# Neighbourhood attention in column order: 416 keys for each query tile, values permuted through a DRAM scratch

## The chip, the cores and the metric

The kernel runs on one core of a Trainium2 chip, as one launch. A core has five engines with instruction queues of their own: TensorE (PE; its weight loads are listed apart as PEld), VectorE (DVE), ScalarE (ACT), GpSimd (POOL) and SyncE (SP). Matmuls write PSUM, which the kernel divides into eight banks of 128 x 512 fp32; everything else lies in SBUF or in DRAM. Transfers are issued from SP's queue and, fewer, from ACT's. The metric is the device time of one execution in microseconds, as the median of several runs.

## The reference

A two-layer diffusion backbone on 256 latent tokens and 256 context tokens of width 2048. Layer 0 projects both through one wide matrix and runs 16 heads of two-dimensional neighbourhood attention beside a bidirectional state-space (SSD) mixer of 8 groups; both are gated, concatenated (4096 wide) and projected back. Layer 1 is a gated short convolution. The part that the change touches is the attention:

```python
rows = seq // GRID_W                       # 256 / 64 = 4 rows of 64 columns
kh = min(NA_KH, rows)                      # 4: every row is in the window
col_start = jnp.clip(col - NA_KW // 2, 0, GRID_W - NA_KW)          # NA_KW = 16
in_win = (col[None, :] >= col_start[:, None]) & (col[None, :] < col_start[:, None] + NA_KW)
...
s_lat = jnp.einsum('bqhd,bkhd->bhqk', qr, kb) * scale + bias        # bias from rpb: row and column distance
s_lat = jnp.where(mask, s_lat, -jnp.inf)
s_ctx = jnp.einsum('bqhd,bkhd->bhqk', qr, k_ctx) * scale
pr = jax.nn.softmax(jnp.concatenate([s_lat, s_ctx], axis=-1), axis=-1)
out = pr[..., :latent] @ vb + pr[..., latent:] @ v_ctx
```

A query in column c sees all four rows of 16 columns around c, and all 256 context tokens. Tokens are numbered row by row: token = 64 * row + column.

## The kernel before

**Precision.** Matrix products are made of three passes: each operand is split into a high part, rounded to the format that TensorE reads fast (fp32r), and the remainder, and high x high, high x low and low x high are added in one bank. `mm` (line 195) issues a matmul, `turn` (line 199) a transpose by a matmul against the identity. Weights come from DRAM in pieces of 512 KB into one of five `raw` buffers (lines 381, 383, on SP), ACT rounds a piece to its high part (line 420), DVE subtracts for the low part (line 427) and frees the buffer; three places hold split weights ahead of TensorE.

**The order of the work.** The program is generated by a planner (class `Plan`): every emitted instruction advances a model of each engine's time. The projections are emitted in a fixed order as the main line of TensorE. All else is generators in three lists, `urgent`, `side` and `back`. A generator yields what it needs next (an engine, the data, a number of banks), and `pump` resumes it when the model says that this would be ready; `may` demands for TensorE that the data be due 0.7 us before the model's present (800 ns less 100), so that matmuls of the side work stand in TensorE's queue only where they should not have to wait. Every engine works its queue in the order emitted, so a wrong guess of the model is a real wait. The model books a DMA at 450 ns of the issuing queue; it lands, from SP, after 1000 ns, its bytes at 270 a ns and 1000 ns more, and from ACT after 1000 ns, its bytes and 2500 ns. A task also needs room in a budget of nine 128 x 512 temporaries.

**The attention.** Heads come in four groups `a` of four. Projections of Q, K, gate and V of a group are followed by those of an SSD group pair: for groups 1 and 2 the order is Q, K, gate, V, SSD, and for group 3 it is Q, K, SSD, gate, V, and then the output projection. Group 0's K and V are summed over eight stages at the start, V in place in `Vt` (line 789).

- `kq_gen`: per 128 tokens, norm, transpose into a bank (4 heads x 128 tokens), ACT writes the high part to `KT` or `QT` (lines 994, 998), DVE the low part to `KL` or `QL` (lines 996, 1000). `KT` and `KL` hold, for each head, 256 latent and then 256 context tokens.
- `v_gen`: when the heads of the group before are done, copies V of the 512 tokens from four banks to `Vt` (line 1012).
- `head_gen`, one for each head: loads the head's bias (four DMAs from a DRAM table `rpbs`, which one DMA builds before, line 929), adds the column mask (line 1044), and for each of two query tiles of 128 tokens scores all 512 keys (three matmuls of 512 columns), adds bias and takes the maximum (line 1057), exponentiates with the sum (line 1062), and scales (lines 1066, 1067). Then it transposes the probabilities, splits them into `PH` and `PL` (lines 1099, 1101), waits for V and the gate, splits its 128 columns of V (`VH`, line 1110, `VL`, line 1112), runs 12 matmuls of 256 columns, and multiplies by the gate (line 1122). `PH` and `PL` exist once, so a head transposes only after the value product of the head before.
- `put_mix` keeps the result for the output projection: in a DRAM scratch `mixd`, or, late in the kernel, at once as split tiles (lines 944, 946). `mix_gen` loads from the scratch and splits (lines 1557, 1561, 1562).

The first pass of the output projection reads 16 pairs of such results with two column blocks, 24 matmuls of 512 columns a pair, in the order 0 to 5, 8 to 15, 6, 7: the last SSD group is pair 15 and comes fourteenth, the heads of group 3 are pairs 6 and 7 and come last.

Of the kernel before, what the change touches and what calls it, by code (L numbers as in the profile page):

```python
# [141 lines left out]
def kernel(ctx: ExitStack, tc, x, cx, ada0, w0, adaT, w_in, w_out, sc_in, sc_out, rpb, small, const,  # L142
# [15 lines left out]
    def drt(shape, name):  # L158
        return dr.tile(list(shape), F32, name="dram_" + name)
# [48 lines left out]
    def spawn(q, gen, tmps=0, halves=0):  # L208
        q.append(Task(gen, tmps, halves))
# [142 lines left out]
    ident, strip, mask, mhalf = C_("ident"), C_("strip"), C_("mask"), C_("mhalf")  # L352
# [561 lines left out]
    got.add(("V", 0))  # L914
# [43 lines left out]
    attn = [0]  # L958

    def kq_gen(key, a, ps, nt, stat, dst, low, banked):  # L960
# [23 lines left out]
        for t in range(nt):  # L984
# [7 lines left out]
            if key == "K":  # L992
                give(free_t, kns[t])
                E(S.copy(dst[:, :, o], four(pt)))
                yield W_("DVE", dst[:, :, o])
                E(V.tensor_tensor(out=low[:, :, o], in0=four(pt), in1=dst[:, :, o].bitcast(F32), op=ALU.subtract))
            else:
                E(S.mul(dst[:, :, o], four(pt), gqk))
                yield W_("DVE", dst[:, :, o])
                E(V.scalar_tensor_tensor(out=low[:, :, o], in0=four(pt), scalar=gqk, in1=dst[:, :, o].bitcast(F32),  # L1000
                                         op0=ALU.mult, op1=ALU.subtract))
                give(free_t, kns[t])
# [3 lines left out]
    def v_gen(a, ps):  # L1006
# [7 lines left out]
        got.add(("V", a))  # L1014
# [14 lines left out]
    b0 = rpbs[0, :, :]  # L1029
# [3 lines left out]
    def head_gen(a, h):  # L1033
# [4 lines left out]
        for r in range(4):  # L1038
            E(DMA.dma_start(bt[64 * (r % 2):64 * (r % 2) + 64, r // 2, :].rearrange("p (a b) -> p a b", a=4),
                            bass.AP(tensor=b0.tensor, offset=b0.offset + hd * 64 * 320 + (7 - r) * 31 - 61,  # L1040
                                    ap=[[319, 64], [31, 4], [1, 64]])))
        yield W_("DVE", bt)
        bv = bt[:, 0:2, :].rearrange("p q (r c) -> p (q r) c", c=64)
        E(V.tensor_tensor(out=bv, in0=bv, in1=mask.unsqueeze(1).to_broadcast([128, 8, 64]), op=ALU.add))
        sps = {}

        def score(qt):
            ps = bank()
            o = slice(qt * 128, (qt + 1) * 128)
            mm(ps, QT[:, h, o], KT[:, h, :], True, False)  # L1050
            mm(ps, QT[:, h, o], KL[:, h, :], False, False)
            mm(ps, QL[:, h, o], KT[:, h, :], False, True)
            return ps

        def top(qt, ps):
            sp = sps[qt] = tmp()
            E(V.tensor_tensor_reduce(out=two(sp), in0=two(ps), in1=bt[:, 1:3, :] if qt else bt[:, 0::2, :], scale=1.0,
# [57 lines left out]
        for kt in range(4):  # L1115
            mm(po[:, :256], VH[:, kt], PH[:, kt, :], kt == 0, False)
            mm(po[:, :256], VH[:, kt], PL[:, kt, :], False, False)
            mm(po[:, :256], VL[:, kt], PH[:, kt, :], False, kt == 3)
# [3 lines left out]
        E(V.tensor_tensor(out=o, in0=po[:, :256], in1=gt[:, h, :], op=ALU.mult))  # L1122
# [358 lines left out]
    Btm[0] = st([128, 2, 4, 128], "Btm", name="Btmt")  # L1481
    spawn(urgent, kq_gen("K", 0, parK, 4, statk, KT, KL, False), 4)
# [570 lines left out]
```

## Time and profile before

| | |
|---|---|
| median of 3 runs | 1762.85 us (1761.52 to 1763.02) |
| profiled execution | 1760.31 us, of which the span of instructions is 1758.5 us |
| PE busy | 1736.7 us, 99% |
| PEld busy | 1463.1 us, 83% |
| DVE busy | 1223.6 us, 70% |
| ACT busy | 773.4 us, 44% |
| DMA | 377.66 MB, mean 215 GB/s |
| granted TensorE clock | 0.999 |

In the rows, `L195` is line 195 of the kernel; a group reads line, engine, operation, `out<-in` by the program's names without buffer numbers, shapes, count, then busy us and the mean duration in ns, then the engine's idle time before the group and what ended it. A row of waits gives the total, the number and the longest wait in us. A row of a timeline or of the chain gives the start in us from the span's start, the length in us, and the work. In rows of DMA issues the last number is the median time in us from issue to landing; `SPq` and `ACTq` are the sequencers that issue.

### The profile page before, as it was taken

Reading aid. Unit: us, or ns where it says so; the run is one execution under the profiler, and the core shown is the slowest. Engines: PE = TensorE matmul, PEld = TensorE weight load, DVE = VectorE, ACT = ScalarE, POOL = GpSimd, SP = SyncE. Lnnn points to the kernel's source line nnn. Section 1 sums busy time; section 2 is a strip of 40 time slices with the busy share of each in tenths; the row PEclk is TensorE's granted clock in tenths of the full one; section 3 lists DMA queues with packets and bytes.
Section 4 is the critical chain, followed back from the end, with each engine's and each line's share of the span. In section 5 each row is a group of like instructions: output and inputs, shape, how many; then the busy total and the mean of one; then the engine's idle time right before and its main releaser. Section 6 shows DMA issues by size and latency. Waiting matters only on the chain.

```text
span 1758.5 us, 25025 instructions
## 1 busy us (share of the span) xinstructions
PE 1736.7 (99%) x9451; PEld 1463.1 (83%) x9451; DVE 1223.6 (70%) x1978; ACT 773.4 (44%) x1330; POOL 31.6 (2%) x28
## 2 busy tenths in 40 slices
PE   6999999999999999999999999999999999999998
PEld 4777988889888889888888898888888888888887
DVE  5666887878685878686877787787668555555554
ACT  5333544445242436343435343564446444444442
POOL 0000100001000000000000000000000000000000
PEclk9999999999999999999999999999999999999999
DMA  9987644686756767656776557768767666666563
GB/s 362 342 307 258 209 143 138 183 246 191 234 165 195 219 205 227 210 175 210 220 213 193 166 185 255 246 221 284 274 222 228 195 188 192 192 191 188 190 208 121
DMA packets 202536, 377.66 MB, mean 215 GB/s; under 512 B 32384, under 2 KB 69040, under 8 KB 202416
## 3 DMA queue, kind: packets, MB, share of 16 engines
q1 hardware_dynamic: 195152, 369.49, 65.5%
q10 hardware_dynamic: 7264, 6.58, 1.1%
q8 instruction: 74, 1.21, 0.3%
q14 instruction: 46, 0.38, 0.1%
HBM read 370.62 MB, written 6.71 MB: 215 GB/s over the span
## 4 chain that ended last, share of the span: by engine, by line
PE 94%; DMA 2%; DVE 2%; issue 1%; ACT 0%; POOL 0%; SPq 0%; ACTq 0%; DVEq 0%; POOLq 0%
PE bank L195 91%; PE bank L199 3%; DMA tmp<-dram_csr 1%; DVE w L427 1%; DMA raw<-in_ada 0%; DMA tmp<-dram_exr 0%; DMA raw<-in_adaT 0%; DVE tmp L1235 0%; ACT w L420 0%; POOL statk L572 0%; DVE mix L1562 0%; SPq L583 0%; DVE raw L823 0%; DVE tmp L603 0%; DVE Vt L1012 0%
## 5 line engine op out<-in xcount | busy, mean ns | idle before, releaser
L420 ACT CAST w<-raw 128x1024 fp32r<-128x1024 f32 x343 | 359.5, 1049 | 530.4 <-PE bank L195 447.7
L427 DVE TENSOR_TENSOR w<-raw,w 128x1024 fp32r<-128x1024 f32 x343 | 416.6, 1217 | 231.4 <-ACT w L420 230.1
L195 PE MATMUL bank<-hH,w 128*128 128x256 f32 (+1 forms) x2064 | 488.0, 324 | 1.2 <-DVE w L427 1.1
L195 PE MATMUL bank<-w,hH 128*128 128x512 f32 x1280 | 407.4, 396 | 2.7 <-ACT hH L757 2.5
L195 PEld LDWEIGHTS bank<-hH,w 128*128 128x128 f32 x2064 | 344.7, 188 | 34.2 <-DVE w L427 2.1
L195 PE MATMUL bank<-hL,w 128*128 128x256 f32 (+1 forms) x1040 | 334.3, 321 | 0.0
L195 PEld LDWEIGHTS bank<-w,hH 128*128 128x128 f32 x1280 | 237.7, 189 | 54.4 <-issue 4.0
L195 PE MATMUL bank<-w,hL 128*128 128x512 f32 x640 | 249.9, 391 | 0.1
L195 PEld LDWEIGHTS bank<-hL,w 128*128 128x128 f32 x1040 | 196.3, 189 | 14.9
L195 PE MATMUL bank<-w,h 128*128 128x512 f32 x768 | 179.7, 390 | 0.0
L823 DVE CUSTOM_DVE_ANT_0 raw<-raw,csb 128x1024 f32<-128x1024 f32 x128 | 155.4, 1219 | 26.2 <-DMA raw<-in_adaT 24.0
L195 PEld LDWEIGHTS bank<-w,h 128*128 128x128 f32 x768 | 143.6, 188 | 29.6
L195 PEld LDWEIGHTS bank<-w,hL 128*128 128x128 f32 x640 | 120.5, 188 | 25.4 <-DVE hL L763 0.6
L195 PE MATMUL bank<-w,mix 128*128 128x512 f32 x588 | 138.3, 391 | 0.9 <-DVE w L427 0.9
L195 PEld LDWEIGHTS bank<-w,mix 128*128 128x128 f32 x588 | 109.5, 188 | 24.0 <-DVE w L427 1.3
L1235 DVE SCALAR_TENSOR_TENSOR tmp<-bank,cwh,tmp 128x508 f32<-128x508 f32 (+1 forms) x96 | 71.0, 744 | 1.8
L195 PE MATMUL bank<-KL,h 128*128 128x512 f32 x264 | 63.8, 389 | 0.0
L427 DVE TENSOR_TENSOR KL<-raw,KL 128x1024 fp32r<-128x1024 f32 x32 | 39.1, 1223 | 33.1 <-ACT KL L420 33.1
L427 DVE TENSOR_TENSOR wL<-raw,wH 128x1024 fp32r<-128x1024 f32 x31 | 37.9, 1224 | 33.5 <-ACT wH L420 33.4
L427 DVE TENSOR_TENSOR QL<-raw,QT 128x1024 fp32r<-128x1024 f32 x32 | 39.2, 1224 | 29.8 <-ACT QT L420 29.8
L195 PEld LDWEIGHTS bank<-KL,h 128*128 128x128 f32 x264 | 49.5, 188 | 10.2
L195 PE MATMUL bank<-QT,h 128*128 128x512 f32 x168 | 56.2, 391 | 0.0
(291 smaller groups left out, 1984.7 us busy)
## 6 DMA issues: line engine op xcount, KB each, us to landing
raw<-in_w_in SPq DMA_DIRECT2D x196, 512.0 KB, 3.9
raw<-in_adaT SPq DMA_DIRECT2D x128, 512.0 KB, 4.8
raw<-in_sc_in SPq DMA_DIRECT2D x128, 512.0 KB, 3.8
raw<-in_w_out SPq DMA_DIRECT2D x64, 512.0 KB, 5.0
raw<-in_ada SPq DMA_DIRECT2D x34, 512.0 KB, 6.9
raw<-in_sc_out SPq DMA_DIRECT2D x32, 512.0 KB, 4.1
PT<-in_ada SPq DMA_DIRECT2D x16, 512.0 KB, 6.9
raw<-in_w SPq DMA_DIRECT2D x16, 512.0 KB, 6.1
```

What stands on the lines that cost most here:

```text
L195: E(T.matmul(o, l, r, start=start, stop=stop, skip_group_check=True))
L199: E(T.transpose(o, i, ident if k == 128 else ident[:k, :k]))
L420: E(S.copy(H, v))
L427: E(V.tensor_tensor(out=Lo, in0=v, in1=H.bitcast(F32), op=ALU.subtract))
L823: E(V.tensor_tensor_reduce(out=raw, in0=raw, in1=csb, scale=1.0, scalar=0.0, op0=ALU.mult, op1=ALU.add, accum_out=gp[:, h, m:m + 1]))
L1235: E(V.scalar_tensor_tensor(out=do, in0=di, scalar=cwh[:, 32 * k + ch:32 * k + ch + 1], in1=do, op0=ALU.mult, op1=ALU.add))
```

## The change

Attention sees the tokens column by column: position = 4 * column + row. A tile of 128 queries is then 32 columns of the grid, not two rows. The 32 columns of tile 0 have windows in columns 0 to 39, those of tile 1 in columns 24 to 63. Keys are laid out as 128 positions of columns 0 to 31, 256 context tokens, and 128 positions of columns 32 to 63, so that each tile's keys are one run of 416: positions 0 to 415, or 96 to 511. What is outside gets probability zero by a memset.

- `kq_gen` writes K and Q to their positions: ACT and DVE read a transposed tile and write elements four apart (two pieces for a latent K tile; DVE in two pieces for a Q tile).
- V has tokens on partitions, so its permutation goes through DRAM: `turn_v` writes the two latent tiles to a scratch `vd` with four DMAs on ACT's queue, waits, and reads them back in the new order with one DMA on SP's queue. Only then is V marked as ready.
- The bias comes as a ready table of 128 x 672 a head from the host (an input with the same numbers in another order), with one DMA a head in place of four; the DRAM table `rpbs`, its DMA and two memsets go. The mask is added in three places where columns can be outside the window.
- The value product multiplies the same four key blocks in another order; the gate product reads its result with a stride of four, which puts tokens back in row order.

```diff
@@ constants @@
-for _name, _w in (("ident", 128), ("sel", 2), ("mhalf", 32), ("strip", 384), ("mask", 64)):
+for _name, _w in (("ident", 128), ("sel", 2), ("mhalf", 16), ("mid", 16), ("strip", 384), ("mask", 64)):
@@ after the first stage, group 0 @@
-    got.add(("V", 0))
...
-    rpbs = drt([16, 64, 320], "rpbs")
-    E(DMA.dma_start(rpbs, bass.AP(tensor=rpb.tensor, offset=76, ap=[[465, 16], [0, 64], [1, 320]])))
+    vd = drt([256, 512], "vd")
     dcol = P_("dcol")
-    for b_ in bias:
-        E(G.memset(b_[:, 2, :], 0.0))
...
+    def columns(ap, t):
+        return ap.rearrange("p h (c r) -> p h r c", r=4)[:, :, 2 * t:2 * t + 2, :]
+
+    def turn_v(a):
+        for t in range(2):
+            for r in range(2):
+                yield W_("AQ", Vt[:, t, :])
+                E(DMA2.dma_start(vd.rearrange("(c r) n -> c r n", r=4)[:, 2 * t + r, :], Vt[64 * r:64 * r + 64, t, :]))
+        yield W_("SP", vd)
+        E(DMA.dma_start(Vt[:, 0:2, :], vd.rearrange("(t p) n -> p t n", p=128)))
+        got.add(("V", a))
@@ kq_gen @@
-                E(S.copy(dst[:, :, o], four(pt)))
-                yield W_("DVE", dst[:, :, o])
-                E(V.tensor_tensor(out=low[:, :, o], in0=four(pt), in1=dst[:, :, o].bitcast(F32), op=ALU.subtract))
+                if t < 2:
+                    places_ = [(columns(dst[:, :, 384 * k:384 * k + 128], t), columns(low[:, :, 384 * k:384 * k + 128], t),
+                                pt.rearrange("p (h r c) -> p h r c", h=4, c=64)[:, :, :, 32 * k:32 * k + 32]) for k in range(2)]
+                else:
+                    o = slice(t * 128 - 128, t * 128)
+                    places_ = [(dst[:, :, o], low[:, :, o], four(pt))]
+                for dh_, _, i in places_:
+                    E(S.copy(dh_, i))
+                yield W_("DVE", dst)
+                for dh_, dl_, i in places_:
+                    E(V.tensor_tensor(out=dl_, in0=i, in1=dh_.bitcast(F32), op=ALU.subtract))
             else:
-                E(S.mul(dst[:, :, o], four(pt), gqk))
...
+                dh_, dl_ = columns(dst, t), columns(low, t)
+                i = pt.rearrange("p (h r c) -> p h r c", h=4, c=64)
+                E(S.mul(dh_, i, gqk))
+                yield W_("DVE", dst)
+                for r in range(2):
+                    E(V.scalar_tensor_tensor(out=dl_[:, :, r], in0=i[:, :, r], scalar=gqk, in1=dh_[:, :, r].bitcast(F32),
+                                             op0=ALU.mult, op1=ALU.subtract))
@@ v_gen @@
-        got.add(("V", a))
+        yield from turn_v(a)
@@ head_gen @@
-        for r in range(4):
-            E(DMA.dma_start(bt[64 * (r % 2):64 * (r % 2) + 64, r // 2, :].rearrange("p (a b) -> p a b", a=4),
...
+        bf = bt.rearrange("p a b -> p (a b)")[:, :672]
+        E(DMA.dma_start(bf, rpb[hd]))
         yield W_("DVE", bt)
-        bv = bt[:, 0:2, :].rearrange("p q (r c) -> p (q r) c", c=64)
-        E(V.tensor_tensor(out=bv, in0=bv, in1=mask.unsqueeze(1).to_broadcast([128, 8, 64]), op=ALU.add))
+        for o_, m_ in ((0, mask[:, 0:32]), (304, mid), (544, mask[:, 32:64])):
+            n_ = m_.shape[-1]
+            bv = bf[:, o_:o_ + 4 * n_].rearrange("p (c r) -> p c r", r=4)
+            E(V.tensor_tensor(out=bv, in0=bv, in1=m_.unsqueeze(2).to_broadcast([128, n_, 4]), op=ALU.add))
         sps = {}
+        span = lambda qt: slice(96 * qt, 96 * qt + 416)
@@ score: the same for the three products @@
-            mm(ps, QT[:, h, o], KT[:, h, :], True, False)
+            mm(ps[:, :416], QT[:, h, o], KT[:, h, k_], True, False)
@@ top @@
+            E(V.memset(sp[:, 0:96] if qt else sp[:, 416:512], 0.0))
+            b_ = bass.AP(tensor=bf.tensor, offset=bf[:, 336 * qt:].offset, ap=[bf.ap[0], [128, 2], [1, 208]])
+            sc = sp[:, span(qt)]
...
-            E(S.activation(sp, sp, AF.Exp, bias=s4[:, 2 + qt:3 + qt], scale=1.0, accum_out=s4[:, 4 + qt:5 + qt]))
+            E(S.activation(sc, sc, AF.Exp, bias=s4[:, 2 + qt:3 + qt], scale=1.0, accum_out=s4[:, 4 + qt:5 + qt]))
@@ scale_ @@
-            sp = sps[qt]
+            sp = sps[qt][:, span(qt)]
@@ value product @@
-        for kt in range(4):
-            mm(po[:, :256], VH[:, kt], PH[:, kt, :], kt == 0, False)
...
+        for i, (kt, vt, q_) in enumerate(BLOCKS):
+            mm(po[:, q_], VH[:, vt], PH[:, kt, q_], i == 0, False)
...
-        E(V.tensor_tensor(out=o, in0=po[:, :256], in1=gt[:, h, :], op=ALU.mult))
+        E(V.tensor_tensor(out=rows4(o), in0=po[:, :256].rearrange("p (c r) -> p r c", r=4), in1=rows4(gt[:, h, :]),
+                          op=ALU.mult))
@@ start of the generators @@
+    spawn(urgent, turn_v(0))
     spawn(urgent, kq_gen("K", 0, parK, 4, statk, KT, KL, False), 4)
```

More of the change, by code (lines that the diff above doesn't have):

```diff
@@ L2021 @@
     const = np.concatenate([
-        np.eye(128, dtype=np.float32), one((j[:, None] % 32) == np.arange(2)[None]), np.full((128, 32), -0.5, np.float32),
-        le, o, le.T, np.where(ok, 0, -1e30).astype(np.float32)], axis=1)
+        np.eye(128, dtype=np.float32), one((j[:, None] % 32) == np.arange(2)[None]), np.full((128, 16), -0.5, np.float32),
+        ok[0, :, 32:40], ok[1, :, 24:32], le, o, le.T, ok[0, :, :32], ok[1, :, 32:]], axis=1)
     strict = np.stack([lt.T, lt], axis=1)
```

34 lines of the change are left out of this document (18 added, 16 removed).

## The prediction

> **What bounds the kernel now.** I read the page's busy times and its chain first, then PE's waits, then a table of stages, and last the attention's own instructions. The first rows are the span, the busy time of each engine, and the chain that ended last.
>
> ```profile
> span 1758.5 us, 25025 instructions
> ## 1 busy us (share of the span) xinstructions
> PE 1736.7 (99%) x9451; PEld 1463.1 (83%) x9451; DVE 1223.6 (70%) x1978; ACT 773.4 (44%) x1330; POOL 31.6 (2%) x28
> ...
> PE 94%; DMA 2%; DVE 2%; issue 1%; ACT 0%; POOL 0%; SPq 0%; ACTq 0%; DVEq 0%; POOLq 0%
> ```
>
> TensorE is busy for 99% of the span and carries 94% of the chain. Whether its work is only stretched is told by what it waits for. These are all of PE's waits after the first 195 us, where the attention and everything behind it lies, and then the table of stages (length; busy time of each engine; granted clock; DMA share; GB/s).
>
> ```profile
> PE bank L195 <- DVE w L427: 2.0, 3, 0.9
> PE bank L199 <- POOL r L1664: 0.3, 1, 0.3
> ```
>
> ```profile
> 195.00:479.00 284.00, 282.92 (x1706) 248.83 (x1705) 220.78 (x397) 134.48 (x297) 12.29 (x6) 1.00 0.64 195
> 479.00:742.00 263.00, 262.93 (x1498) 227.68 (x1498) 195.14 (x333) 111.13 (x215) 7.21 (x4) 1.00 0.65 201
> 742.00:1121.00 379.00, 379.00 (x2172) 329.85 (x2171) 290.61 (x494) 161.91 (x304) 6.30 (x4) 1.00 0.67 208
> 1121.00:1210.00 89.00, 88.09 (x453) 73.46 (x451) 73.21 (x136) 51.32 (x90) 1.39 (x2) 1.00 0.74 240
> ```
>
> The stages end where V of head groups 1, 2 and 3 is copied; in all four PE is busy for over 98%, at full clock, while DVE is busy for 74 to 82% and DMA for 64 to 74%. So a column that TensorE need not stream is worth its full time here, other engines' work is worth nothing while it is on time, and only 2.3 us of PE waits are left to win.
>
> **Part 1: the scores (on the path).** 16 heads x 2 query tiles x 3 products are 96 matmuls, and each falls from 512 to 416 columns. A matmul's recorded duration contains its pipeline, so its price is the step from one start to the next. The first fence is a piece of the chain that holds only 512-column matmuls; the next two rows are the first and last of one head's 12 value matmuls (256 columns).
>
> ```profile
> 1535.03 43.54 PE bank L195 x192
> ```
>
> ```profile
> 1129.19 0.28 PE L195 MATMUL bank<-PH,VH 128*128 128x256 f32 x1
> ...
> 1130.48 0.28 PE L195 MATMUL bank<-PH,VL 128*128 128x256 f32 x1
> ```
>
> 43.54 / 192 = 0.2268 us for 512 columns, and 1.29 us / 11 steps = 0.1173 us for 256. That is 0.428 ns a column; 96 columns are 41.1 ns, and 96 matmuls save 3.9 us. Bounds: if 416 columns cost as much as 512, nothing; if time went with columns alone (0.2268 x 96 / 512 = 42.5 ns), 4.1 us. I take 3.9, because the value matmuls, each with its own weights, show that steps well below 0.19 us are reached. The other TensorE work of a head stays: 8 transposes (zeros fill the 96 columns) and 12 value matmuls of 256 columns, the four key blocks only in another order.
>
> **Part 2: softmax, masks and copies on DVE and ACT (beside PE).**
>
> ```profile
> L420 ACT CAST w<-raw 128x1024 fp32r<-128x1024 f32 x340 | 357.6, 1053 | 528.7 <-PE bank L195 447.7 <-issue 52.2 <-DVE gp L823 8.8
> ...
> L994 ACT CAST KT<-bank 128x512 fp32r<-128x512 f32 x16 | 9.0, 590 | 10.2 <-PE bank L199 10.2
> ```
>
> ```profile
> L1067 DVE TENSOR_SCALAR tmp<-tmp,s 128x512 f32<-128x512 f32 x32 | 15.6, 487 | 1.1
> ...
> L1057 DVE CUSTOM_DVE_ANT_0 tmp<-bank,bias 128x512 f32<-128x512 f32 x16 | 11.0, 686 | 2.5 <-PE bank L195 2.5
> ...
> L1122 DVE TENSOR_TENSOR half<-bank,gt 128x256 f32<-128x256 f32 x16 | 6.7, 421 | 11.9 <-PE bank L195 11.8
> ...
> L523 DVE COPY cpad<-csil 128x16 f32<-128x16 f32 x1 | 0.2, 181 | 0.0
> ...
> L590 DVE TENSOR_SCALAR bs<-small 128x16 f32<-128x16 f32 x1 | 0.2, 167 | 0.0
> ```
>
> The columns behind the bar are busy us and mean ns of one, then the idle time before them. Two-input DVE work costs (686 - 421) / 256 = 1.04 ns an element, so the max pass saves 0.10 us and the scaling pass at most as much: about 6 us over 32 tiles. New are 32 memsets of 96 elements (between the 0.17 us of the smallest operation above and 0.42: 5 to 13 us; 5, nearer the 16-element rows), two more mask operations a head on 320 instead of 512 elements (about even, up to +0.2 us x 16), and one more subtraction a tile for 8 K and 8 Q tiles (2 x 421 - 686 = +0.16 us, 2.5 us). DVE ends some 2 to 13 us busier, in four stages of 1015 us in which it now idles for 235. ACT's casts give (1053 - 590) / 512 = 0.90 ns an element; it saves 96 x 0.90 x 32 = 2.8 us in the exponentials, and pays for 8 more K copies and 16 DMA issues. PE would meet this only through weight splits (L420, then L427) that come late; those waits are the 2.0 us above. So: nothing, with those waits grown as the end that I can't bound from here.
>
> The K, Q and bias forms change too. Columns of K and Q are written 16 bytes apart. The nearest row is L523, a 16-element write at 128 bytes apart: 181 ns against 167 contiguous, so 0 to 0.9 ns more per element. At 0.9, two K tiles of 512 elements give 0.9 us on ACT and the last subtraction 0.5 us on DVE, 1.4 us for a group.
>
> ```profile
> 423.89 0.68 DVE L996 TENSOR_TENSOR KL<-bank,KT 128x512 fp32r<-128x512 f32 x1
> ...
> 426.72 0.40 PE L195 MATMUL bank<-KT,QT 128*128 128x512 f32 x1
> ```
>
> In group 1 the last K subtraction ends at 424.57 and the first score starts at 426.72, so 2.1 us cover it: nothing on the path. [...]
>
> **Part 3: values through DRAM (new latency).**
>
> ```profile
> raw<-in_w_out SPq DMA_DIRECT2D x64, 512.0 KB, 5.0
> ...
> tmp<-dram_csr SPq DMA_DIRECT2D x32, 256.0 KB, 5.9
> bias<-dram_rpbs SPq DMA_DIRECT2D x64, 64.0 KB, 3.7
> ...
> dram_mixd<-half ACTq DMA_DIRECT2D x24, 128.0 KB, 3.1
> ...
> dram_rpbs<-in_rpb SPq DMA_DIRECT2D x1, 1280.0 KB, 9.7
> ```
>
> ```profile
> 1118.96 0.37 ACTq L1557 DMA_DIRECT2D tmp<-dram_mixd  x1
> ...
> 1120.32 1.07 ACT L1012 COPY Vt<-bank 128x512 f32<-128x512 f32 x2
> ...
> 1125.71 0.62 ACT L1110 CAST VH<-Vt 128x512 fp32r<-128x512 f32 x1
> ```
>
> Four writes of 128 KB issue on ACT's queue, 3 x 0.37 us apart, and land 3.1 us after issue; then SP issues one 512 KB read (0.4, as ACT's issue) that lands after 5.0: 9.6 us from V's copies to V in column order, 10.5 with the 5.9 us of the csr loads. The kernel's planner books the same trip as 3 x 0.45 + 3.99 for the writes, and 3.94 for the read: 9.3 us. It puts a matmul in PE's order only 0.7 us after its inputs are due (800 less 100 ns), so PE meets lateness above 0.7 us; 0.3 us at these rows costs nothing.
>
> What queues behind the new waits: on SP, weight loads behind the read that waits for the writes (it is issued when the planner thinks them landed); on ACT, weight casts behind the four issues (1.5 us a group) and behind L1110, which waits for V. Both have three places of split weights ahead of PE; loads that are late shrink that lead first. Where V comes later, so do four heads.
>
> ```profile
> L789 DVE TENSOR_TENSOR Vt<-Vt,bank x28: 676/681/687, 67.5 to 189.9; 128x512 f32<-128x512 f32 x28
> L1110 ACT CAST VH<-Vt x16: 611/624/635, 265.4 to 1164.4; 128x512 fp32r<-128x512 f32 x16
> ```
>
> Group 0's V is complete at 190.6 and first cast at 265.4: 75 us to spare. Groups 1 and 2 have most of their stages of 263 and 379 us before the next group's V. Group 3 is tight: L1110 at 1125.71 would move to about 1131.0 (1121.4 + 9.6), 5.3 us later. The tail that follows it:
>
> ```profile
> 1198.72 0.70 ACT L944 CAST mix<-half 128x256 fp32r<-128x256 f32 x2
> ...
> 1200.00 0.76 DVE L946 TENSOR_TENSOR mix<-half,mix 128x256 fp32r<-128x256 f32 x2
> ```
>
> ```profile
> 1115.00:1203.10 88.10, 74.21 (x312) 57.88 (x313) 8.11 (x22) 7.23 (x20) 1.00 0.73 239
> ```
>
> The second row counts the output projection's matmuls alone: 312 are 13 pairs of 24, so the fourteenth pair starts at 1203.1. It reads the last SSD group, done at 1200.8: 2.3 us ahead. That group doesn't read V, and heads that come later leave it DVE and ACT earlier; the heads themselves are read from the fifteenth pair on, 5.4 us later still. I cost the tail at nothing, with 5.3 - 2.3 = 3.0 us as the other end, if the SSD group moves as far as the heads.
>
> SP loses 65 issues (64 bias pieces, the 1280 KB table copy) and gains 20. DMA loses about 6.7 MB (4.2 bias, 2 x 1.3 copy) and gains 5.5 MB of bias and 4.2 of V: 3 MB more of 378, at a share of 64 to 74%. POOL loses two memsets. All at nothing; the covers are the DMA's free quarter and SP's waits for free buffers.
>
> **The sum.** -3.9 (scores) + 0 (K, Q) + 0 (trip) + 0 (tail) = -3.9 us. The profiled execution took 1760.31 us (span 1758.5, 1.8 around it), so 1756.4 for its like; the median of the runs is 2.5 above it, 1762.85 - 3.9 = 1758.95, say 1759.0. A difference of 0.2% (3.5 us) is about what a measurement of this kernel tells from no change, and the forecast clears that by only 0.4 us.
>
> **Rivals.**
> *The tail waits.* The last SSD group ends with the delayed heads and PE stands before the fourteenth pair: -3.9 + 3.0, 1761.9. For it: heads and that group share DVE and ACT between 1126 and 1200. Against: the group waits for no V.
>
> *V lands late, and the kernel is slower.* In groups 1 to 3 the first head stands ready when V arrives, so its value matmuls hit PE directly. The chain of waits has a load as slow as this:
>
> ```profile
> 1104.08 7.98 DMA tmp<-dram_csr
> ```
>
> With 8.0 for the read the trip is 12.6 us, 3.3 later than booked, and PE stands 3.3 - 0.7 = 2.6 us three times: -3.9 + 7.8, 1766.7. It decides from 2.5 us of stall a group, (3.9 + 3.5) / 3. For it: DMA shares of 64 to 74% and reads queued behind weight loads. Against: the median rows.
>
> *The strided writes are several times slower.* At four times an element's time, two K tiles add 2 x 512 x 0.90 x 3 = 2.8 us on ACT and 512 x 1.04 x 3 = 1.6 on DVE; less 2.1 of cover, 2.3 us in each of four groups: -3.9 + 9.2, 1768.2. L523 speaks against it. [...]
>
> *The shorter scores take as long as before*, for example by a weight load of 188 ns each: 1762.9. The steps of 0.1173 us speak against it.
>
> **How the numbers follow.** Forecast 0.48 clear of the bound and 0.04 just short of it (a little of the 3.9 given back); tail 0.22; V late 0.17; strides 0.04; scores no shorter 0.05. Faster 0.48, same 0.04 + 0.22 + 0.05 = 0.31, slower 0.21. The low end takes the 2.0 us of PE waits on weights as gone too and 0.4 for the runs' spread: 1756.5. The high end leaves out the upper half of the slower cases, 0.1: 1766.0. The likeliest case by itself lies at 1756.5 to 1759.3.
>
> **What would show it.** Score matmuls of 416 columns, 0.186 us from start to start; PE's waits after 195 us still near 2 us; a new PE wait on the value split (L1112's place) if V is late, on the mixes' split near 1200 if the tail waits, and on K's or Q's low part if strides are slow; the strided copies' own durations against 0.59 us for two halves; the writes to the scratch and the read of it near 3.1 and 5.0 us. The prediction is wrong if the re-planned order, which moves every instruction behind 195 us a little, makes weight splits late in places that none of these terms names.

## The result, and the profile after

The changed kernel takes 1785.43 us (median of 4 runs, 1783.53 to 1786.53), the kernel before beside it 1762.18 us (4 runs): a ratio of 1.0129, 95% interval 1.0109 to 1.0149. It is 23 us slower, where 1759.0 was forecast and 1756.5 to 1766.0 was the range. Line numbers below are those of the changed kernel, unless another is named.

The first rows of the page after, which answer to those of before (span, busy time of each engine, granted TensorE clock in 40 slices):

```profile
span 1781.7 us, 25097 instructions
## 1 busy us (share of the span) xinstructions
PE 1741.7 (98%) x9451; PEld 1467.8 (82%) x9451; DVE 1226.7 (69%) x2058; ACT 776.6 (44%) x1338; POOL 33.9 (2%) x26
...
PEclk9999999999999999999999999998999999999999
```

DVE is 3.1 us busier and ACT 3.2. PE is still the bound. What stands out is the one slice of 44.5 us with a lower clock (from 1203 to 1247 us), and that PE's share fell from 99 to 98% of a longer span. Where it waits, behind 195 us, is the next view (total, times, longest, times in us), in place of the two rows of 2.0 and 0.3 us before:

```profile
PE bank L195 <- DVE w L427: 6.6, 4, 2.7
PE bank L195 <- DVE half L1477: 4.1, 1, 4.1
PE bank L199 <- DVE KL L1014: 3.1, 1, 3.1
PE bank L199 <- POOL r L1490: 2.8, 2, 1.7
PE bank L195 <- DVE tmp L1448: 1.8, 2, 1.2
PE bank L195 <- ACT mix L940: 1.0, 1, 1.0
PE bank L195 <- DVE QL L1021: 0.4, 1, 0.4
PE bank L199 <- DVE tmp L985: 0.2, 1, 0.2
```

They add up to 20.0 us. Only L427, 6.6 us of it, is a weight split. The others belong to the side work: the norm and the low parts of K and Q (L985, L1014, L1021), and with L1448, L1477, L1490 and L940 the steps of an SSD group. They lie in two places, which the table of stages shows (length; busy time of PE, PEld, DVE, ACT and POOL; granted clock; DMA share; GB/s):

```profile
195.00:479.00 284.00, 274.56 (x1660) 241.35 (x1660) 220.89 (x427) 134.53 (x296) 14.87 (x6) 0.99 0.60 190
...
1121.00:1230.00 109.00, 98.40 (x474) 80.66 (x473) 78.42 (x156) 54.57 (x102) 1.40 (x2) 0.94 0.69 236
```

PE idles for 9.4 us in the first stage and for 10.6 in the last. In the two stages between, 479 to 1121 us, it isn't idle at all. Behind the waits stands a second loss. Between 195 us and the end of this table, three stretches have a granted clock of one half (busy time of PE alone, then clock, DMA share, GB/s):

```profile
242.20:245.60 3.40, 3.40 (x13) 0.51 0.86 294
1133.10:1136.50 3.40, 3.40 (x10) 0.50 0.71 221
1218.50:1228.70 10.20, 6.14 (x17) 0.50 0.80 277
```

Taken as half, 12.9 us of work at half clock lose 6.5 us. That is an estimate: in the second stretch 512-column matmuls start 0.43 us apart (1133.44, 1133.87, 1134.29, 1134.72), against 0.2268 at full clock in the kernel before, which gives 6.1. The account: waits 20.0 - 2.3 = 17.7, half clock 6.5, scores -3.8 (next), together 20.4 of the 23.2 us by which the span grew. For the other 2.8 us there is no row.

The scores themselves came out as forecast. These are the three score matmuls of one query tile and the first value matmul behind them (start, length):

```profile
336.31 0.35 PE L195 MATMUL bank<-KT,QT 128*128 128x416 f32 x1
336.49 0.35 PE L195 MATMUL bank<-KL,QT 128*128 128x416 f32 x1
336.68 0.35 PE L195 MATMUL bank<-KT,QL 128*128 128x416 f32 x1
336.87 0.28 PE L195 MATMUL bank<-PH,VH 128*128 128x256 f32 x1
```

0.56 / 3 = 0.187 us a step (forecast 0.186), against 0.2268 before: 96 x 0.040 = 3.8 us saved.

The trip of V is where the trace differs from the plan. The transfers themselves are somewhat slower than the 3.1 and 5.0 us of the forecast (count, KB each, median us from issue to landing):

```profile
dram_vd<-Vt ACTq DMA_DIRECT2D x16, 128.0 KB, 4.4
Vt<-dram_vd SPq DMA_DIRECT2D x4, 512.0 KB, 5.6
```

But they aren't issued when they could be. For group 3 the timeline of ACT and of SP has these rows (start, length, engine, line, work, and in brackets the idle time ahead and what ended it):

```profile
1131.02 1.11 ACTq L965 DMA_DIRECT2D dram_vd<-Vt  x2
...
1136.91 1.05 ACT L420 CAST w<-raw 128x1024 fp32r<-128x1024 f32 x1 [3.58 <-PE bank L195]
1139.67 1.05 ACT L420 CAST w<-raw 128x1024 fp32r<-128x1024 f32 x1 [1.71 <-PE bank L195]
...
1142.40 1.10 ACTq L965 DMA_DIRECT2D dram_vd<-Vt  x2
...
1161.86 0.62 ACT L1136 CAST VH<-Vt 128x512 fp32r<-128x512 f32 x1 [3.76 <-DMA Vt<-dram_vd]
```

```profile
1154.14 0.65 SPq L967 DMA_DIRECT2D Vt<-dram_vd  x1
```

The second pair of writes stands 11.4 us behind the first, though nothing in the data holds it, and the read 11.7 us behind that. The first cast of V starts 31 us after the first write is issued; the forecast had 9.6 us for the whole trip. In between ACT is busy for only 10.52 of the 24 us from 1131 to 1155: beside a few splits of mixes it does little but weight casts, each as soon as PE frees a place.

### The profile page after: what moved, and what is told of

The parts are those of the page before. It is cut to its first block, busy times and chain, and to the rows that moved or that the text cites. A ratio compares the mean times of both kernels' runs of the same rounds, so it can differ in the third digit from the quotient of the medians.

```text
span 1781.7 us, 25097 instructions
## 1 busy us (share of the span) xinstructions
PE 1741.7 (98%) x9451; PEld 1467.8 (82%) x9451; DVE 1226.7 (69%) x2058; ACT 776.6 (44%) x1338; POOL 33.9 (2%) x26
## 2 busy tenths in 40 slices
DMA packets 188761, 381.86 MB, mean 214 GB/s; under 512 B 15536, under 2 KB 51168, under 8 KB 188640
## 4 chain that ended last, share of the span: by engine, by line
PE 92%; DVE 3%; DMA 3%; ACT 1%; issue 1%; POOL 0%; SPq 0%; ACTq 0%; DVEq 0%
PE bank L195 88%; PE bank L199 3%; DMA tmp<-dram_csr 1%; DVE w L427 1%; DMA tmp<-dram_mixd 0%; DMA raw<-in_ada 0%; DMA bias<-in_rpb 0%; DVE raw L823 0%; POOL statk L572 0%; DVE mix L1591 0%; DVE tmp L1443 0%; DVE QL L1021 0%; ACT w L420 0%; ACT QT L1018 0%; DVE tmp L1432 0%
## 5 line engine op out<-in xcount | busy, mean ns | idle before, releaser
L427 DVE TENSOR_TENSOR w<-raw,w 128x1024 fp32r<-128x1024 f32 x343 | 415.9, 1217 | 222.7 <-ACT w L420 220.0
L823 DVE CUSTOM_DVE_ANT_0 raw<-raw,csb 128x1024 f32<-128x1024 f32 x128 | 155.9, 1220 | 51.4 <-DMA raw<-in_adaT 48.2
L195 PE MATMUL bank<-w,mix 128*128 128x512 f32 x588 | 142.2, 399 | 4.2 <-DVE w L427 3.1
L427 DVE TENSOR_TENSOR KL<-raw,KL 128x1024 fp32r<-128x1024 f32 x32 | 39.2, 1224 | 32.7 <-ACT KL L420 32.6
L427 DVE TENSOR_TENSOR QL<-raw,QT 128x1024 fp32r<-128x1024 f32 x32 | 39.2, 1224 | 31.4 <-ACT QT L420 31.4
L427 DVE TENSOR_TENSOR wL<-raw,wH 128x1024 fp32r<-128x1024 f32 x31 | 38.0, 1224 | 32.6 <-ACT wH L420 32.5
L195 PEld LDWEIGHTS bank<-KL,h 128*128 128x128 f32 x264 | 49.5, 188 | 10.2
```

The lines of the kernel that those rows point to most:

```text
L195: E(T.matmul(o, l, r, start=start, stop=stop, skip_group_check=True))
L427: E(V.tensor_tensor(out=Lo, in0=v, in1=H.bitcast(F32), op=ALU.subtract))
L823: E(V.tensor_tensor_reduce(out=raw, in0=raw, in1=csb, scale=1.0, scalar=0.0, op0=ALU.mult, op1=ALU.add, accum_out=gp[:, h, m:m + 1]))
```

## What the planner believed

The order of the instructions is the planner's, so its own times of the trip matter (us of the model's time, as the program is generated, for each group: ACT's time ahead of the first write, ACT's time behind the fourth, with a little other work of ACT in it, and when V is due):

```
            changed kernel               rows of the scratch kept apart
group 0     232.5   249.7   259.6        232.5   234.3   246.6
group 1     539.7   552.3   562.7        532.7   534.5   543.4
group 2     815.0   827.6   838.2        808.2   810.0   820.4
group 3    1204.9  1228.9  1241.2       1194.0  1199.8  1212.8
```

The planner notes for each DRAM tensor which range of 256-element units an access spans, from its first element to its last. Each of the four writes takes every fourth row of `vd`, so the ranges of all four overlap nearly wholly. `add` (line 98) starts a write no earlier than 60 ns after the last write to the same unit has landed. So each of the four is booked to *start* only when the one before has landed, 3 to 5 us later (or 11, where transfers are queued ahead), and ACT's time in the model moves along: 12.6 to 24 us a group in place of 1.8 (5.8 in group 3). On the chip the DMAs are issued without such a wait: the pair above is out within 1.11 us. But `may` gives out ACT work only while ACT's modelled time is less than 4.5 us ahead of PE's, so for all that time no side work is given to ACT. (The margin of 0.7 us by which a matmul of the side work stands behind its data holds for the lists `side` and `back` alone, line 267. Tasks in `urgent`, the transposes of K and Q among them, go without it.) The theory to test is this:

**Theory 1, the false booking:** ACT counts as busy, the work of heads and SSD groups is emitted late, and PE meets it at fixed points of its main line. **Rival A, the strided writes:** K and Q written 16 bytes apart delay the scores. **Rival B, the late V:** the heads crowd together, whoever booked what. **Rival C:** the trip itself, its DMAs and queues.

## The experiments

**Take each suspect away.** Four kernels, each the changed one with one or two things undone. The first changes the planner alone and the DMAs' work not at all:

```diff
@@ Plan.keys @@
+        if "vd" in n:
+            one = a[0][1] == 64
+            return [(n, ap.offset // 512 % 4)] if one else [(n, u) for u in range(4)]
         hi = ap.offset + sum(abs(s) * (c - 1) for s, c in a)
```

> The changed kernel, but the planner's bookkeeping knows the four rows of the scratch apart. As changed, it books the four writes of V one after the other (4 us each on ACT's time), because their interleaved rows overlap as ranges, and so issues the read late: the trip takes 22 to 31 us in the trace in place of 9.6. Theory 1 (the late V of the last head group moves the tail): the read is issued some 10 us earlier, the wait before the fourteenth pair near 1214 to 1224 us goes, and the time falls by about 13 us to 1772. Theory 2 (the strided K and Q writes, slower than booked, cost it): nothing changes, 1785.

Measured: 1757.01 us (8 runs, 1756.42 to 1760.67), ratio to the kernel before 0.9967 (0.9953 to 0.998). That is 28.4 us less than the changed kernel. The whole loss is gone, and the kernel is 6.1 us faster than the kernel before in the same set of runs (1763.11 us), or 3.6 us by the spans of the profiled executions (1754.9 against 1758.5). It lies within the range that was forecast for the change. PE's waits behind 195 us, and the same trip of group 3 (lines are 3 further on):

```profile
PE bank L198 <- DVE w L430: 2.3, 3, 1.0
PE bank L202 <- POOL r L1696: 0.3, 1, 0.3
PE bank L198 <- DVE tmp L1345: 0.2, 1, 0.2
```

```profile
1116.92 1.11 ACTq L968 DMA_DIRECT2D dram_vd<-Vt  x2
...
1119.97 0.62 ACTq L968 DMA_DIRECT2D dram_vd<-Vt  x1
...
1136.15 0.62 ACT L1139 CAST VH<-Vt 128x512 fp32r<-128x512 f32 x1 [0.97 <-DMA Vt<-dram_vd]
```

Four writes within 3.1 us (one more lies between the rows), and V cast 19 us after the first of them. That is still twice the 9.6 us of the forecast; what it costs, the third run below tells.

The second writes K and Q contiguously (so its scores are of other keys), the trip as it is:

```diff
-                if t < 2:
-                    places_ = [(columns(dst[:, :, 384 * k:384 * k + 128], t), columns(low[:, :, 384 * k:384 * k + 128], t),
-                                pt.rearrange("p (h r c) -> p h r c", h=4, c=64)[:, :, :, 32 * k:32 * k + 32]) for k in range(2)]
-                else:
-                    o = slice(t * 128 - 128, t * 128)
-                    places_ = [(dst[:, :, o], low[:, :, o], four(pt))]
+                places_ = [(dst[:, :, o], low[:, :, o], four(pt))]
...
-                E(S.mul(dh_, i, gqk))
+                E(S.mul(dst[:, :, o], four(pt), gqk))
```

> The changed kernel with K and Q written contiguously, in row order (so its scores are of other keys and its output is not the reference's); everything else, the trip of V included, stays. Theory 2: the stalls behind the K and Q copies near 211 and 239 us and the half-clock window behind them go, some 7 to 10 us, to 1776; copies return to 0.37 and 0.59 us. Theory 1: the tail stays, so 1780 to 1785.

Measured: 1772.03 us (7 runs, 1765.87 to 1776.42), ratio 1.0047 (1.0027 to 1.0066). 13 us better than the changed kernel, below what either theory was expected to give, and still worse than before. (The edit does a little more than move the writes: there are fewer and larger copies and subtractions, and DVE waits only for the piece just written.)

The third counts V as there at once (V stays in row order), and leaves the strided writes:

```diff
-        yield from turn_v(a)
+        got.add(("V", a))
```

> The changed kernel without the trip: V is marked ready where it was before (V stays in row order, so the output is not the reference's); strided K and Q writes stay. Theory 1: the tail is back, 13 us or more go, 1772 or less. Theory 2: 1783 or more.

Measured: 1756.09 us (5 runs, 1755.69 to 1757.71), ratio 0.9954 (0.9937 to 0.997).

The fourth does both:

> Both taken away: contiguous K and Q writes and no trip (neither output is the reference's); what is left of the change is the scores of 416 columns, the bias table, the masks and the memsets. If trip and strides are the whole loss, the forecast saving of 3.9 us appears: 1758. If a changed order of the side work alone makes stalls (a third theory), it stays above 1765.

Measured: 1759.65 us (10 runs, 1758.06 to 1764.68), ratio 0.9979 (0.9967 to 0.9992).

What follows: with no trip, strided writes are no slower than contiguous ones (1756.09 against 1759.65, if anything the other way), so rival A falls as a cause by itself. A real trip with honest bookkeeping costs about 1 us against none (1757.01 against 1756.09): rival C falls as the cause of 23 us. Why contiguous writes win 13 us while the false booking is there, and lose 3.6 without it, isn't settled. Either they cost only where the lead is gone, or the new order of all instructions happened to be a better or a worse one. For the first speaks that PE's waits on K's low part near 240 us, 3.1 us in the changed kernel, are 2.0 us in the contiguous one; for the second, that its other large waits lie at other places (up to 675, 677, 981, 1142 and 1152 us) and the last SSD group makes PE wait no more.

**The trip without the rest of the change.** The kernel before, with the trip added, once with the planner as it is and once with the rows kept apart:

```diff
@@ the kernel before @@
+    vd = drt([256, 512], "vd")
...
-        got.add(("V", a))
+        yield from turn_v(a)
...
+    spawn(urgent, turn_v(0))
```

> The kernel before with one addition: V still goes through the scratch and comes back in column order (four writes, one read, as in the changed kernel), while scores, K, Q, bias and masks stay as before; the value product then multiplies probabilities by permuted rows of V, so the latent part of the attention is another sum, of the same cost. The planner is as in the changed kernel, and takes the four interleaved writes for writes to the same place. Theory 1 (the planner books the trip at 23 to 36 us and ACT as busy for 12 of them): clearly slower than before, by some 10 to 28 us, 1772 to 1790, with the waits of PE on weight splits and the late last SSD group of the changed kernel. Rival (the loss needs the column order too: more, smaller instructions on DVE and ACT and the trip together): within 4 us of before, 1759 to 1767.

> As the run with the trip alone, but the planner keeps the four row sets of the scratch apart. Theory 1: the real trip costs nothing, 1762 plus or minus 3. Rival (the trip itself costs, and column order hid it elsewhere): 1767 or more.

Measured: 1791.92 us (4 runs, 1786.14 to 1795.87), ratio 1.0149 (1.011 to 1.0188), and 1766.47 us (10 runs, 1762.72 to 1767.93), ratio 1.0012 (0.9996 to 1.0028). The first is a little above the 1772 to 1790 of Theory 1. The second lies outside its 1762 plus or minus 3 and just under the 1767 of the rival; the kernel before stood at 1764.07 in this set of runs, so the real trip comes out 2.4 us above no trip (-0.7 to 4.9 by the interval), which doesn't tell a cost of a few us from none. The difference of the two is clear: the column order isn't needed for the loss, and the booking makes 25 us of it here too.

**Booking without a trip, lateness without a booking.** Theory 1 and rival B were still one: the false booking also makes V late. So one kernel advances only the planner's time of ACT, with V there at once, and one holds V back for 25 us of the planner's time and books nothing. Neither has a DMA of the trip:

```diff
@@ turn_v, booking alone @@
+        got.add(("V", a))
+        land = 0.0
+        for k in range(4):
+            yield W_("AQ", Vt[:, k // 2, :])
+            s = max(plan.t["ACT"], land + 60)
+            plan.t["ACT"] = s + 450
+            land = max(plan.dma, s + 1000) + 131072 / 270 + 2500
@@ turn_v, late V alone @@
+        yield W_("AQ", Vt[:, 0, :], Vt[:, 1, :])
+        t0 = plan.t["PE"]
+        yield when(lambda: plan.t["PE"] >= t0 + 25000)
+        got.add(("V", a))
```

> The changed kernel without any DMA of the trip; V counts as there at once (so V isn't permuted, and the latent part of the attention is another sum), but the planner's time of ACT is advanced in four steps of about 4 us as the changed kernel's planner does. This is the false booking of ACT alone. If the false booking of ACT is what costs (ACT stands idle while the planner thinks it busy, and weight splits lose their lead): most of the 28 us between 1757 and 1785, that is 1770 to 1785. If the late V is what costs: 1756 to 1760.

> The changed kernel without any DMA of the trip, where V counts as there only 25 us of the planner's PE time after its copies are ready (V isn't permuted, and the latent part of the attention is another sum); no time of ACT is booked. This is the late V alone. If the late V costs (heads and last SSD group crowd into the time before the output projection's fourteenth pair): most of the loss, above 1768, with PE waits at 1200 to 1225. If the false booking of ACT costs: 1756 to 1762.

Measured: 1782.34 us (4 runs, 1781.31 to 1782.96), ratio 1.0097 (1.0058 to 1.0136), and 1756.75 us (10 runs, 1755.04 to 1758.74), ratio 0.9959 (0.9943 to 0.9974). That separates them. V is really late in the second: in group 3 its first cast starts at 1144.2 us, 22 us later than where V counts as there at once (1122.1). PE's waits behind 195 us, with the booking alone (the four largest) and with the late V alone:

```profile
PE bank L199 <- POOL r L1490: 4.1, 2, 2.1
PE bank L195 <- DVE w L427: 4.0, 3, 2.7
PE bank L199 <- DVE KL L1014: 3.1, 1, 3.1
PE bank L195 <- DVE half L1477: 3.0, 1, 3.0
```

```profile
PE bank L195 <- DVE w L427: 2.0, 3, 0.8
PE bank L195 <- ACT w L420: 1.0, 1, 1.0
```

The first are the waits of the changed kernel, the same lines and nearly the same sizes, though no DMA of a trip is left in the program and nothing has been put in its place. ACT's busy time in the two stretches where trips stand (length; busy; clock; DMA share; GB/s), booking alone and then late V alone:

```profile
195.00:220.00 25.00, 15.11 (x58) 1.00 0.79 245
1131.00:1155.00 24.00, 11.18 (x17) 0.93 0.68 223
```

```profile
195.00:220.00 25.00, 19.92 (x66) 1.00 0.60 188
1131.00:1155.00 24.00, 15.81 (x32) 1.00 0.83 254
```

Nearly 5 us of ACT's work are put off each time, and PE meets them later: at the low part of K (237 us), at the end of the first SSD group (400 us) and at the end of the last one. The last result of that group (L1477) starts at 1218.2 us with the booking, at 1186.0 with the late V (its L1474), at 1220.0 in the changed kernel and at 1192.2 in the kernel before (its L1449). Part of that is the main line's own lateness by then: 13 pairs of the output projection are done at 1213.7 us in the changed kernel and at 1203.1 in the kernel before.

**Which groups.** The same booking for group 0 alone and for group 3 alone:

```diff
+        if a != 0:          # or 3
+            return
         land = 0.0
```

> As the run with ACT's false booking alone, but only for head group 0, behind the summed stages; groups 1 to 3 book nothing. V isn't permuted, so the latent part of the attention is another sum. By the places of the stalls in that run (236 to 244, 390 to 422: about 8 us, with 3.4 us at half clock), group 0 alone costs about 11 us: 1765 to 1770, and TensorE stands at the same places, not behind 1120. If the bookings only hurt by adding up from group to group: below 1760.

> As the run with ACT's false booking alone, but only for head group 3, the last one before the output projection. V isn't permuted, so the latent part of the attention is another sum. By the places of the stalls in that run (1128, 1141, 1212 to 1222: about 12 us, with 3 to 10 us at half clock), group 3 alone costs 12 to 17 us: 1768 to 1775, with the last SSD group late and nothing lost before 1120. If the bookings only hurt by adding up from group to group: below 1760.

Measured: 1768.52 us (9 runs, 1766.9 to 1770.68), ratio 1.0029 (1.0019 to 1.004), and 1767.19 us (10 runs, 1764.83 to 1769.52), ratio 1.0015 (1.0004 to 1.0027). Against the 1756.75 of the late V alone that is 11.8 and 10.4 us, and with 25.6 for all four groups, groups 1 and 2, and what the bookings do to one another, have about 3 left. Group 3 was expected a little dearer (12 to 17 us). Groups 0 and 3 are those with the largest false bookings (17 and 24 us in the changed kernel, not 12.6). That they also have a fixed point of PE's main line close behind (the first scores and SSD group, and the output projection's fourteenth pair) is an argument, not a measurement.

**The gain by itself.** The kernel with known rows, its scores over all 512 keys again:

```diff
-            mm(ps[:, :416], QT[:, h, o], KT[:, h, k_], True, False)
+            mm(ps, QT[:, h, o], KT[:, h, :], True, False)
...
-            E(V.tensor_tensor_reduce(out=two(sc), in0=two(ps[:, :416]), in1=b_, scale=1.0,
+            E(V.tensor_tensor_reduce(out=two(sc), in0=two(ps[:, span(qt)]), in1=b_, scale=1.0,
```

> The changed kernel with the planner knowing the rows of the scratch, and one part of the change undone: each query tile scores all 512 keys again (three matmuls of 512 columns), and the maximum and all behind it still take only the tile's 416. Part 1 of the prediction: 96 x 96 columns more at 0.428 ns, 3.9 us more than the 1757.0 us (span 1754.9) of the run with known rows: 1760.9, span 1758.8. Rival (the shorter scores take as long as before): 1757, span 1755.

Measured: 1764.51 us (12 runs, 1763.09 to 1767.56), ratio 1.0007 (0.9997 to 1.0018), span 1761.8: 7.5 us more than with the shorter scores by the medians, 6.9 by the spans, where 3.9 was expected. All of PE's waits behind 195 us in it:

```profile
PE bank L198 <- DVE w L430: 5.4, 5, 2.8
```

That is 2.6 us more than the 2.8 of the kernel with known rows. 6.9 - 2.6 = 4.3 is near the 3.8 of the steps. The 2.6 us are not a price of columns: the planner books 512 columns and so emits another order, and that order has a weight split 2.8 us late.

**What a wait costs.** Last, the half clock. Into the kernel with known rows, in its quiet part behind 1400 us, nine waits of PE were put, by a transpose that reads what a chain of VectorE operations has written:

```diff
+    def stall(n):
+        force(lambda: free_b and free_t)
+        pt, o = bank(), tmp()
+        E(V.memset(o, 0.0))
+        turn(pt[:, :128], ident)
+        E(V.tensor_copy(o[:, :128], pt[:, :128]))
+        for _ in range(n):
+            E(V.tensor_scalar(out=o, in0=o, scalar1=1.0, scalar2=0.0, op0=ALU.mult, op1=ALU.add))
+        turn(pt[:, 128:256], o[:, :128])
...
+                if kb == 8 and (i, part) in STALLS:
+                    stall(STALLS[i, part])
```

> The changed kernel with known rows, and nine waits of TensorE of set lengths in the quiet part after 1350 us: each time a small transpose, 1, 3, 5, 7, 11, 19, 2, 4 and 9 operations of about 0.49 us on VectorE, and a transpose that waits for them (waits of some 1.5 to 10 us, 35 to 40 us together). It prices a wait by itself. If a wait costs its length and then a stretch at half clock (as after the waits of 2.9 us and more in the changed kernel: windows of 3.4 us and once 10.2, so 1.7 to 5 us lost each): the waits from about 2.9 us on are followed within 5 us by a stretch of granted clock 0.5, those of 2 us and less by none, and the time is 1757 plus the waits plus some 10 to 20 us, near 1805 to 1815. If a wait costs its length alone: no such stretch, near 1792 to 1797.

Measured: 1805.26 us (4 runs, 1804.17 to 1807.54), 48.2 us more than without the waits. They came out at 1.0, 1.9, 2.9, 3.7, 5.6, 9.3, 1.5, 2.35 and 4.7 us, in the order of the kernel, and the view of PE's waits behind 1350 us gives for them:

```profile
PE bank L202 <- DVE tmp L1966: 32.9, 9, 9.3
```

The other 15 us are mostly half clock: six stretches, of which these are the first and the longest, with 25.3 us of PE's work in all (34 us long), so 12.7 us lost by the same estimate as above.

```profile
1454.90:1458.30 3.40, 3.40 (x9) 0.51 0.69 199
...
1656.30:1666.50 10.20, 5.69 (x14) 0.50 0.18 51
```

But the expectation put the bound at the wait's length, 2.9 us, and that is wrong. The waits of 1.9 and 2.35 us were followed by half clock, the one of 2.9 us (2.86) was not. All stretches start on one grid of 3.41 us (1454.9, 1553.9, 1601.7, 1656.3, 1734.8 and 1762.1 us: 29, 14, 16, 23 and 8 steps apart; those of the changed kernel, at 242.2, 1133.1 and 1218.5 us, lie 261 and 25 such steps apart), and what tells the cells apart here is how much PE works within one. These are the cells of the 1.9 us wait, of the 2.9 us wait (which falls across two), and of the 2.35 us wait:

```profile
1451.50:1454.90 3.40, 1.51 (x9) 1.00 0.76 219
1499.30:1502.70 3.40, 1.99 (x10) 1.00 0.72 194
1502.70:1506.10 3.40, 1.96 (x9) 1.00 0.29 109
...
1731.40:1734.80 3.40, 1.04 (x6) 1.00 0.93 277
```

1.51 of 3.40 us (44%) and less was followed by a cell at half clock, 1.96 (58%) and more wasn't. Cells of 3.41 us, laid over the changed kernel behind 200 us, bear it out: the cells ahead of its three stretches hold 0.31, 0.70 and 0.65 us of work, and of the cells at full clock that half clock doesn't follow, the least holds 1.8 us (from 402.6 us). So over the cells read in both kernels the bound lies between 1.51 and 1.8 us, near half a cell. In the changed kernel the cells at half clock that held 1.0 and 1.7 us (from 1218.5 us) were followed by another at half clock, and the three that full clock followed were busy throughout. A cell in which PE still worked for 44% of the time was enough here.

## Why the prediction was wrong, point by point

- **The step that failed** is in part 3: "The kernel's planner books the same trip as 3 x 0.45 + 3.99 for the writes, and 3.94 for the read: 9.3 us." It books 23 to 36 us. I had worked with its prices of one DMA and not with its rule on who must wait for whom: four interleaved row sets are one range to it. I took ACT's share as "the four issues (1.5 us a group)"; the planner took it as 12.6 to 24 us a group, and a planner that thinks an engine busy leaves it idle. So the term "0 (trip)" of the sum was really some 25 us. The run with the booking alone shows that this suffices for nearly all of the loss (1782.34 of 1785.43, where 1756.75 stands without it).
- **V late, the rival on the slower side** had the right sign and the wrong mechanism. It put three waits of 2.6 us at the value matmuls of groups 1 to 3. No PE wait of the changed kernel stands there, and V 25 us late costs nothing that can be told (1756.75 against 1756.09), since heads have that slack in every group, in group 3 too. It priced its waits at 7.8 us; the loss against the kernel with known rows is 28.4 and sits elsewhere. That the kernel came out slower, as this rival had it, is luck.
- **The tail at nothing, 3.0 at the other end:** the place was right, the last SSD group ahead of the fourteenth pair, and the size wrong. It came 28 us late (L1477 at 1220.0 against 1192.2), of which the main line, 10.6 us late itself, gave back only a part. PE stood there, and lost more by 10.2 us at half clock. "That group doesn't read V" was true and beside the point: it needs ACT.
- **Scores, -3.9:** right. Steps of 0.187 us, 3.8 us. Undone alone it showed 6.9 us of span, 2.6 of it in weight splits that the new order made late. A difference of a few us between two kernels thus holds their orders as much as their columns, and that the kernel with known rows came out 2.0 us under the forecast is no closer a test than this.
- **K and Q written 16 bytes apart, nothing on the path:** right by the run without a trip. The sign that the prediction named for slow strides, a PE wait on K's low part, did come in the changed kernel (3.1 us), but not for that reason alone: with the same strided writes and no false booking it is gone. Part 2 gave 0 to 0.9 ns more per element. The rows show the upper end and a little above it. These are Q's high part, K's low part, K's high part, and a contiguous ACT copy of 256 elements from a bank, then Q's high part in the kernel before (mean ns behind the comma):

```profile
L1018 ACT ACTIVATE QT<-bank,gqk 128x512 fp32r<-128x512 f32 x8 | 9.3, 1184 | 7.3 <-PE bank L199 7.3
...
L1014 DVE TENSOR_TENSOR KL<-bank,KT 128x256 fp32r<-128x256 f32 x16 | 9.3, 631 | 2.1 <-ACT KT L1011 2.1
...
L1011 ACT CAST KT<-bank 128x256 fp32r<-128x256 f32 x16 | 8.5, 667 | 6.9 <-PE bank L199 6.9
...
L724 ACT COPY half<-bank 128x256 f32<-128x256 f32 x16 | 6.0, 373 | 53.9 <-PE bank L195 53.9
```

```profile
L998 ACT ACTIVATE QT<-bank,gqk 128x512 fp32r<-128x512 f32 x8 | 5.5, 690 | 10.9 <-PE bank L199 10.9
```

  (1184 - 690) / 512 = 0.96 and (667 - 373) / 256 = 1.15 ns more on ACT, (631 - 421) / 256 = 0.82 on DVE (421 ns is the mean of the gate product, which also takes 256 elements of a bank and a second operand): about twice the time of an element, not the four times that the rival assumed, and hidden. That the spacing of the writes, and not another part of the new forms, makes these nanoseconds is not shown by a run.
- **DVE, ACT and DMA beside PE:** right in the sum, DVE 3.1 us busier (2 to 13 was given). DMA moved 4.2 MB more (381.86 against 377.66), not 3.
- **What the prediction named as its weak point**, "the re-planned order ... makes weight splits late in places that none of these terms names", is the nearest it came to the cause, though only 6.6 of the 20.0 us of waits are weight splits. It had no price and no place, though the way to one was open: to follow one strided access through the planner's own bookkeeping.

## What to carry to other kernels

Where a planner decides the order, a new access pattern has two prices: what the chip takes for it and what the planner believes. Follow the new instruction through the planner's dependence rule, not only through its cost formula, because an engine wrongly booked is idle and shows in no busy time. And each of the clock cells of 3.41 us above that waits left with 1.51 us of PE's work or less was followed by a cell at half clock, up to 1.7 us lost by the estimate of half, so waits can be dearer than their sum (48.2 us for the 32.9 us of the last run).

The change is worth having once the planner knows the four row sets apart: 1757.01 us, ratio 0.9967 (0.9953 to 0.998) to the kernel before, with the same work on the chip as the version that was 23 us slower.

## What the runs showed of the hardware that I had not expected

- TensorE's clock went to half for whole cells of a grid of 3.41 us, and did so after a cell with 44% of work (1.51 us). By how they lay on the grid, a wait of 1.9 us was followed by 3.40 us at half clock, some 1.7 us more by the estimate of half, and one of 2.9 us by none.
- The copies and subtractions that write 16 bytes apart took ACT 0.96 to 1.15 and DVE 0.82 ns more per element than the contiguous rows beside them, but the gate product, which reads its bank with a stride of four elements, takes the same 421 ns as before (L1149).
- V may come 25 us of the planner's time late in this kernel with no loss that can be told, while some 5 us of work that ACT is not given in time cost 10 to 12.
